# The last output group of a feed-forward stage moves into the hand-written order, outputs are issued in two parts, and vector work is asked for one turn sooner

## The chip, the cores and the metric

The kernel runs on one core of a Trainium2 chip. The engines named below are TensorE (PE, matrix products), VectorE (DVE), ScalarE (ACT), GpSimd (POOL) and SyncE (SP, which only issues the loads and stores here). The metric is the device time of one execution in microseconds (us). The kernel before takes 1966.19 us, the median of three runs that lie between 1964.42 and 1966.62.

## The reference

Two layers work on 512 latent tokens and 256 context tokens of 1024 channels. Each layer has an attention part (two kinds of attention, gated and projected) and then a feed-forward part. The change touches the feed-forward part alone, which in the reference is

```python
def swiglu(h, w_in, w_out):
    a, u = jnp.split(h @ w_in, 2, axis=-1)
    return (jax.nn.silu(a) * u) @ w_out
...
        h2 = modulate(rms_norm(x, norm2[l]), sh2, sc2)
        x = x + g2 * swiglu(h2, w_ffn_in[l], w_ffn_out[l])
        if not last:
            hc2 = modulate(rms_norm(ctx, norm2[l]), csh2, csc2)
            ctx = ctx + cg2 * swiglu(hc2, w_ffn_in[l], w_ffn_out[l])

    return rms_norm(x, final_norm)
```

`D_FF` is 2816. The first layer runs it over latent and context tokens together (768 columns in the kernel), the second over the 512 latent tokens alone. What follows is a norm: the next layer's first one, or the final one.

## The kernel before

**Numbers.** All data is 32-bit float. A product is made of three matmuls with halved operands: ACT copies a tile to the shorter matmul type (the *hi*), DVE subtracts the hi from the tile (the *lo*), and PE adds hi x hi, lo x hi and hi x lo in one PSUM bank. So every weight that is loaded costs an ACT copy and a DVE subtraction before PE can use it. In the trace the raw weight is `wr`, its halves are `wh` and `wl` (lines 366 and 368 for a weight split by the general helper, 1882 and 1886 for one split in the fixed order) or `w` (lines 1589 and 1593, for the quad's quarters).

**Layout.** Channels lie on the 128 partitions and tokens on the free axis. The 2816 hidden channels are 22 blocks `f` of 128, the 1024 output channels are 8 blocks `j`. The right-hand side, the normed tokens, is held in halves of `nh` columns: 384 in the first layer, 256 in the second.

**Hidden blocks.** `hidden(f)` makes gate and up projection of one block with `quad`, a scheme of Strassen's kind: seven turns of 12 matmuls in place of eight. The turns run in the order A11, A12, S1, S2, S4, S3, A22; their left operands are quarters of the weight or sums of quarters (S1, S2, S3, S4, made by DVE in `Quarters.sum`, lines 2124 to 2133). They use three PSUM banks, u, c, v, in the order u, c, v, u, v, u, u (`qu`, `qc`, `qv`). A bank goes on adding over its turns, and between two of them it must be read: ACT copies u after A11 (p1) and after S2 (u2), and v after S1 (v1), all at line 1732; DVE reads c after A12 (line 2152), v after S4 (again 2152) and u after S3 (line 2165, `tt<-qu,tt`) and after A22 (line 2169). Lines 1869 and 1870 then split the finished hidden block into `ph` and `pl`.

**Outputs.** After each chunk of four hidden blocks, `output` multiplies them with a 128x512 piece of the second weight (`wfo`) for each j, and DVE adds the gated result to the residual, `x<-po,G,x` (line 1581). Columns wider than one bank go in two spans. The last chunk has six blocks (`LAST`), so pieces of 128x768 and loads of 384 KB.

**Order.** In the middle of the feed-forward part, `paced` writes the order of PE, DVE and ACT by hand. It takes a list of steps (the turns and the outputs) and keeps four stages for them, load, sum, hi and lo, each some turns ahead of the step that PE is to run: lo three turns, hi four, sum five. Before it makes the sum of a step it makes sure that the lo of all steps up to two before it are written, because sums are made in place of quarters. The first step after a quad's S3 goes ahead of the quad's A22, so that there is other work between two turns on bank u. Loads go through SP's queue in the order in which they are issued, and hi and lo of an output live in three rotating buffers each.

**The last outputs.** Behind the part with the written order, the scheduler of the compiler's front end sets the order. The last chunk's outputs are made in two column groups (0 to 512 and 512 to 768 in the first layer, 0 to 256 and 256 to 512 in the second). The first group runs j = 0 to 7 and loads and splits one weight for each; the second runs j = 7 to 0, finds the last three weights still in their buffers, and loads and splits the other five again. With each residual a square is made and added up for the norm that follows (lines 484, 487 and 488); in the first layer the first group's x is also stored to `xd`.

## Time and profile before

One execution was profiled. It took 1967.19 us, 1.0 us more than the median; its span, from the first to the last instruction, is 1965.1 us, at a mean granted PE clock of 0.996.

| what | number |
| --- | --- |
| median of three runs | 1966.19 us |
| the profiled execution | 1967.19 us, span 1965.1 us |
| PE busy | 1920.8 us, 98% |
| DVE busy | 1479.8 us, 75% |
| ACT busy | 948.9 us, 48% |
| POOL busy | 220.1 us, 11% |
| loads of `wfo` for the last outputs | 26, 384 KB each, 3.3 us to landing |
| ACT's hi of such a weight, `wh` 128x768 | 26, 840 ns each |
| DVE's lo of such a weight, `wl` 128x768 | 26, 954 ns each |
| residual `x<-po,G,x` 128x512, 128x256 | 72 of 750 ns, 80 of 480 ns |

Times in rows of the trace are start and duration in microseconds, counted from the start of the span. `x12` groups twelve neighbours. What stands in square brackets is how long the engine stood idle ahead of the row, and which instruction ended that by the profile. Matmuls are pipelined: the next one starts before the row before it ends, so a pace is read from start to start. In the span's clock the hidden blocks of the first layer end near 1089, its last outputs run from there to 1138, and those of the second layer start near 1920.

### The profile page before, as it was taken

How to read it: one execution, taken by the hardware profiler on the slowest of the kernel's cores; microseconds unless marked ns; L12 is line 12 of the kernel's file. 1: busy time of each engine (PE TensorE's matmuls, PEld its weight loads, DVE VectorE, ACT ScalarE, POOL GpSimd, SP SyncE). 2: the span in 40 equal slices, each digit the busy share in tenths (PEclk: the TensorE clock that was granted, in tenths of full speed). 3: DMA queues.
4: the chain of work that ended last, by engine and by line, in shares of the span. 5: the costliest groups of instructions: out<-in, count | busy, mean ns of one | idle time of the engine just before them, and what ended most of it. 6: DMA issues, size and time to landing. Idle time of an engine off the chain costs nothing.

```text
span 1965.1 us, 31571 instructions
## 1 busy us (share of the span) xinstructions
PE 1920.8 (98%) x12298; PEld 1777.7 (90%) x12298; DVE 1479.8 (75%) x2813; ACT 948.9 (48%) x1832; POOL 220.1 (11%) x130
## 2 busy tenths in 40 slices
PE   8999999999999999999999999999999999999998
PEld 8989999888899999999999888889888999988997
DVE  7468887788768888786867587879566587876785
ACT  5456666642236534242524255667453364544454
POOL 0332212213200000000000013222300000000000
PEclk9999999999999999999999999999999999999999
DMA  8121112244452143434453422112235532233333
GB/s 324 44 71 41 52 57 63 76 148 166 144 207 86 65 132 127 124 107 138 137 161 116 129 86 60 52 49 78 67 93 196 176 112 77 95 112 96 94 109 108
DMA packets 73109, 214.78 MB, mean 109 GB/s; under 512 B 8704, under 2 KB 10880, under 8 KB 72960
## 3 DMA queue, kind: packets, MB, share of 16 engines
q1 hardware_dynamic: 72960, 212.78, 33.2%
q8 instruction: 96, 1.57, 0.3%
q14 instruction: 53, 0.43, 0.1%
HBM read 200.69 MB, written 6.82 MB: 106 GB/s over the span
## 4 chain that ended last, share of the span: by engine, by line
PE 66%; DVE 6%; issue 3%; ACT 2%; DMA 0%; POOL 0%; DVEq 0%; POOLq 0%; ACTq 0%
PE po L381 19%; PE qu L1726 13%; PE pj L381 10%; PE qv L1726 7%; PE pp L381 4%; PE qc L1726 3%; PE pf L381 3%; PE pv L954 1%; PE sc L1037 1%; PE y L1073 1%; PE tp L1063 1%; PE sc L1164 1%; PE y L1200 1%; DVE w L1593 1%; PE tp L1188 1%
## 5 line engine op out<-in xcount | busy, mean ns | idle before, releaser
L1726 PE MATMUL qu<-r,w 128*128 128x384 f32 (+1 forms) x1872 | 295.4, 310 | 1.9 <-ACT tt L1732 1.9
L1726 PEld LDWEIGHTS qu<-r,w 128*128 128x128 f32 x1872 | 281.1, 189 | 6.5 <-ACT tt L1732 2.7
L381 PE MATMUL pj<-h,wh 128*128 128x512 f32 (+1 forms) x704 | 257.5, 366 | 5.2 <-ACT kg L813 1.7
L366 ACT ACTIVATE wh<-wr 128x1024 fp32r<-128x1024 f32 (+2 forms) x157 | 146.1, 935 | 213.8 <-issue 67.2
L381 PE MATMUL pj<-h,wl 128*128 128x512 f32 (+1 forms) x704 | 247.6, 352 | 0.0
L381 PE MATMUL pj<-hl,wh 128*128 128x512 f32 (+1 forms) x704 | 247.0, 351 | 0.0
L381 PE MATMUL po<-ph,wh 128*128 128x512 f32 (+1 forms) x576 | 197.8, 344 | 2.6 <-ACT wh L366 1.6
L381 PE MATMUL po<-ph,wl 128*128 128x512 f32 (+1 forms) x576 | 196.4, 342 | 2.1 <-DVE wl L368 1.4
L381 PE MATMUL po<-pl,wh 128*128 128x512 f32 (+1 forms) x576 | 195.8, 340 | 0.0
L1589 ACT ACTIVATE w<-wr 128x512 fp32r<-128x512 f32 x234 | 145.4, 625 | 103.5 <-DVE wr L2129 39.3
L368 POOL TENSOR_TENSOR wl<-wr,wh 128x1024 fp32r<-128x1024 f32 (+1 forms) x66 | 144.6, 2194 | 392.8 <-ACT wh L366 392.7
L1581 DVE SCALAR_TENSOR_TENSOR x<-po,G,x 128x256 f32<-128x256 f32 (+3 forms) x168 | 99.1, 596 | 113.4 <-PE po L381 112.4
L1593 DVE TENSOR_TENSOR w<-wr,w 128x512 fp32r<-128x512 f32 x234 | 159.6, 685 | 14.9 <-ACT w L1589 13.6
L1726 PE MATMUL qv<-r,w 128*128 128x384 f32 (+1 forms) x936 | 151.1, 310 | 1.7 <-ACT tt L1732 1.7
L381 PEld LDWEIGHTS pj<-h,wh 128*128 128x128 f32 x704 | 134.0, 190 | 20.2 <-ACT kg L813 1.9
L381 PEld LDWEIGHTS pj<-h,wl 128*128 128x128 f32 x704 | 133.4, 189 | 18.2
L381 PEld LDWEIGHTS pj<-hl,wh 128*128 128x128 f32 x704 | 134.2, 191 | 13.8
L1726 PEld LDWEIGHTS qv<-r,w 128*128 128x128 f32 x936 | 141.1, 190 | 2.8 <-ACT tt L1732 2.7
L1013 ACT ACTIVATE pth<-tp 128x512 fp32r<-128x512 f32 x176 | 103.4, 595 | 65.3 <-PE tp L1063 37.7
L509 POOL TENSOR_TENSOR rs<-rs,expo 128x2 f32<-128x2 f32 (+2 forms) x8 | 6.2, 773 | 1116.7 <-DVE rs L508 1116.7
L1014 DVE TENSOR_TENSOR ptl<-tp,pth 128x512 fp32r<-128x512 f32 x176 | 119.5, 685 | 15.1 <-ACT pth L1013 13.4
L381 PEld LDWEIGHTS po<-ph,wh 128*128 128x128 f32 x576 | 108.4, 188 | 17.5 <-ACT wh L366 3.5
(249 smaller groups left out, 4321.2 us busy)
## 6 DMA issues: line engine op xcount, KB each, us to landing
wr<-wfi SPq DMA_DIRECT2D x88, 512.0 KB, 3.3
wr<-wmodT SPq DMA_DIRECT2D x84, 512.0 KB, 3.3
wr<-win SPq DMA_DIRECT2D x68, 512.0 KB, 3.3
wr<-wfo SPq DMA_DIRECT2D x64, 256.0 KB, 2.7
wr<-wo SPq DMA_DIRECT2D x26, 512.0 KB, 3.6
wr<-wfo SPq DMA_DIRECT2D x26, 384.0 KB, 3.3
wr<-wp SPq DMA_DIRECT2D x32, 256.0 KB, 2.9
x<-x SPq DMA_DIRECT2D x16, 384.0 KB, 6.4
```

The costliest lines, as they stand in the source:

```text
L366: nc.scalar.activation(hi, raw, AF.Copy)
L368: (eng or nc.gpsimd).tensor_tensor(lo, raw, hi[:].bitcast(F32), op=ALU.subtract)
L381: nc.tensor.matmul(ps[:, : b - a], u[:, c], v[k][:, a:b], start=(k == 0 and i == 0), stop=(k == nk - 1 and i == 2),)
L954: nc.tensor.matmul(ps[:, t * 256 : t * 256 + 256], a[k][:, tok], b[:, c], start=(k == 0 and i == 0), stop=(k == KB - 1 and i == 2))
L1013: nc.scalar.activation(hi, tp, AF.Copy)
L1014: nc.vector.tensor_tensor(lo, tp, hi[:].bitcast(F32), op=ALU.subtract)
L1037: nc.tensor.matmul(s[:, lo:up], qt[:, b * P : (b + 1) * P], kk[k][:, lo:up], start=(k == 0 and (b % 2 == 0 or lo > 0)), stop=(k == 1), ski ...
L1063: nc.tensor.transpose(tp[:, (2 * j + b) * P : (2 * j + b + 1) * P], ps_[b][:, (k + j) * P : (k + j + 1) * P], self.ident)
L1581: self.nc.vector.scalar_tensor_tensor(x[j][:, f:u], ps[:, f - a : u - a], self.G[l][i][:, s, j : j + 1], x[j][:, f:u], op0=ALU.mult, op1=A ...
L1589: self.nc.scalar.activation(t[:, :n], src, AF.Copy)
L1593: self.nc.vector.tensor_tensor(t[:, n : 2 * n], src, t[:, :n].bitcast(F32), op=ALU.subtract)
L1726: nc.tensor.matmul(banks[bank], u[:, c], v, start=(first and k == 0 and i == 0), stop=(k == kn - 1 and i == 2), skip_group_check=True)
```

## The change

There are three parts.

1. **When the stages of a step are due.** A table `goal` is made ahead of the loop. The lo is due as before. The hi of a step, and likewise its sum, is due when it was due before, or as soon as the stage after it is due one step later, whichever reaches further. And a stage `sum` of a step that makes no sum no longer forces the lo of the steps before it.

2. **Outputs in parts.** `outward` takes the place of `output`. A span of 512 columns becomes two steps, each with half of the matmuls over the hidden blocks in the same bank; the residual follows the second. The step that goes between S3 and A22 is thus half an output. For the last chunk the first two outputs are cut after 3, 5 and 6 of the six hidden blocks, and the third parts, which need the last hidden block, are put behind.

3. **The last outputs.** The first column group is now part of the steps that `paced` orders. Its weights j = 0 to 4 (`KEPT`) get slots of their own in a larger pool, so all eight are still there for the second group, which loads and splits nothing. The squares are made through `summed`. The second group is written as before, without the loads.

Per layer this takes out five loads of 384 KB, five ACT copies and five DVE subtractions. The matmuls are the same ones.

```diff
--- before.py
+++ after.py
@@ -32,6 +32,8 @@
 FB = FF // P
 
 CHUNK, LAST = 4, 6
+KEPT = 5
 EPS = 1e-6
 QSCALE = -(HD ** -0.5)
 BIG = 3.0e38
@@ -1758,6 +1760,12 @@
         for s in steps:
             at.append(at[-1] + s.cost)
         order = "load", "sum", "hi", "lo"
+        last = len(steps)
+        upto = lambda n, t: max(n + 1, next((i for i in range(n, last) if at[i] >= at[n] + t), last))
+        goal = dict(lo=[upto(n, 3 * near + 0.1) for n in range(last)])
+        for stage, after, t in (("hi", "lo", 4), ("sum", "hi", 5)):
+            goal[stage] = [max(upto(n, t * near + 0.1), goal[after][min(n + 1, last - 1)]) for n in range(last)]
         done = dict.fromkeys(order, 0)
         share = min(1.0, 1.2 * sum(c for c, *_ in beside) / sum(s.cost - s.busy for s in steps))
         free, wait, since = 0.0, [], 0.0
@@ -1767,7 +1775,7 @@
         def go(stage, up):
             while done[stage] < up:
                 n = done[stage]
-                if stage == "sum":
+                if stage == "sum" and steps[n].sum:
                     go("lo", n - 2)
                 if stage != "load":
                     go(order[order.index(stage) - 1], n + 1)
@@ -1793,14 +1801,13 @@
             self.live += 1
 
         for n, s in enumerate(steps):
-            ahead = lambda t: max(n + 1, next((i for i in range(n, len(steps)) if at[i] >= at[n] + t), len(steps)))
             first, late, later = late, later, []
-            go("lo", ahead(3 * near + 0.1))
+            go("lo", goal["lo"][n])
             for run in first:
                 run()
-            go("hi", ahead(4 * near + 0.1))
-            go("sum", ahead(5 * near + 0.1))
-            far = ahead(5 * near + LEAD)
+            go("hi", goal["hi"][n])
+            go("sum", goal["sum"][n])
+            far = upto(n, 5 * near + LEAD)
             while done["load"] < far and (not steps[done["load"]].load or self.live <= 2):
                 go("load", done["load"] + 1)
             free = min(free + (s.cost - s.busy) * (share if ready() else 1.0), BEHIND)
@@ -1869,32 +1876,52 @@
                 lambda: nc.scalar.activation(hi[:, : 2 * nh], src, AF.Copy),
                 lambda: nc.vector.tensor_tensor(lo[:, : 2 * nh], src, hi[:, : 2 * nh].bitcast(F32), op=ALU.subtract)]
 
-        def output(chunk, j):
-            n = CHUNK * P
+        def outward(chunk, j, spans, own=False, then=None, cuts=None):
+            kn = CHUNK if chunk < last_chunk else LAST
+            n = kn * P
             w, banks = {}, {}
 
             def load():
-                w["raw"] = self.raw(d["wfo"][l, j, :, chunk * n : (chunk + 1) * n], n)
+                w["raw"] = self.raw(d["wfo"][l, j, :, chunk * CHUNK * P : chunk * CHUNK * P + n], n)
                 self.live += 1
 
+            def half(tag):
+                return self.slot(tag, F32R) if own else self.wpool.tile([P, n], F32R, tag=tag, name=self.name(tag))
             def upper():
-                w["hi"] = self.wpool.tile([P, n], F32R, tag="wh", name=self.name("wh"))
+                w["hi"] = half("wh")
                 nc.scalar.activation(w["hi"], w["raw"], AF.Copy)
 
             def lower():
-                w["lo"] = self.wpool.tile([P, n], F32R, tag="wl", name=self.name("wl"))
+                w["lo"] = half("wl")
                 nc.vector.tensor_tensor(w["lo"], w["raw"], w["hi"][:].bitcast(F32), op=ALU.subtract)
                 self.live -= 1
 
-            def mul(a, b):
-                banks[a] = self.ps("a", "po")[:, : b - a]
-                drain(self.steps(banks[a], (w["hi"], w["lo"]), second[chunk], a, b, CHUNK))
-            return [
-                Step(3 * CHUNK * ((b - a) * COL + FIX), (0.0 if a else busy(n)) + busy(b - a) + 0.06,
-                     lambda a=a, b=b: mul(a, b), lambda a=a, b=b: self.residual(l, 1, banks[a], x, j, a, b),
-                     gated=True, **({} if a else dict(load=load, hi=upper, lo=lower)))
-                for a, b in spans]
+            def mul(a, b, up):
+                if a not in banks:
+                    ps = self.ps("a", "po")[:, : b - a]
+                    banks[a] = ps, self.steps(ps, (w["hi"], w["lo"]), second[chunk], a, b, kn)
+                for _ in range(up):
+                    next(banks[a][1], None)
+            def take(a, b):
+                self.residual(l, 1, banks[a][0], x, j, a, b)
+                return then(j, a, b) if then else None
+            steps = []
+            for a, b in spans:
+                at = 0
+                for up in cuts or ((kn // 2, kn) if b - a == S else (kn,)):
+                    first, end = not steps, up == kn
+                    cost = busy(n) * first + (busy(b - a) + 0.06 + (busy(b - a) if then else 0.0)) * end
+                    steps.append(Step(
+                        3 * (up - at) * ((b - a) * COL + FIX), cost, lambda a=a, b=b, n=up - at: mul(a, b, n),
+                        (lambda a=a, b=b: take(a, b)) if end else lambda: None, gated=True,
+                        **(dict(load=load, hi=upper, lo=lower) if first else {})))
+                    at = up
+            return steps, w
 
         def rest():
 
@@ -1903,13 +1930,35 @@
             for f in range(len(early) // 2, FB):
                 parts = [hidden(f)]
                 if f % CHUNK == 1 and CHUNK < f < FB - CHUNK // 2:
-                    parts.append([s for j in range(KB) for s in output(f // CHUNK - 1, j)])
+                    parts.append([s for j in range(KB) for s in outward(f // CHUNK - 1, j, spans)[0]])
                 for some in parts:
                     end = some[-1:] if some is parts[0] else []
                     some = some[: len(some) - len(end)]
                     steps += some[:1] + tail + some[1:]
                     tail = end
-            return steps + tail
+            for j in range(KB):
+                some, ws[j] = outward(last_chunk, j, groups[:1], j < KEPT, summed, (3, LAST - 1, LAST) if j < 2 else None)
+                steps += some[:1] + tail + some[1:-1] if j == 0 else some[:-1] if j == 1 else some
+                tail = some[-1:] if j == 0 else []
+                if j == 1:
+                    steps += last + some[-1:]
+                last = some[-1:]
+            return steps
+        def summed(j, a, b):
+            if l < DEPTH - 1:
+                nc.sync.dma_start(self.xd[j][:, a:b], x[j][:, a:b])
+            t = pool.tile([P, S], F32, tag="sq" if acc else "acc", name=self.name("sq"))[:, : b - a]
+            acc.append(t)
+            todo = [(1, lambda: nc.scalar.activation(t, x[j][:, a:b], AF.Square))]
+            if j:
+                todo.append((2, lambda: nc.vector.tensor_tensor(acc[0], acc[0], t, op=ALU.add)))
+            return todo
+        last_chunk = (FB - LAST) // CHUNK
+        ws, acc = {}, []
 
         early, cover = EARLY[l], COVER[l]
         order = [(*part, half) for half in range(2) for part in early[:cover]]
@@ -1930,29 +1979,22 @@
         order = {getattr(mybir.EngineType, e) for e in ("PE", "DVE", "Activation")}
         with self.tc.manual_schedule(engines=order):
             self.paced(rest(), 3 * KB // 2 * (nh * COL + FIX), beside, lambda: self.gated)
-        chunk = (FB - LAST) // CHUNK
-        ws = {}
-        for i, (a, b) in enumerate(groups):
-            acc = None
-            for at, j in enumerate(list(range(KB))[:: 1 - 2 * i]):
-                if i == 0 or at >= 3:
-                    ws[j] = self.weight(d["wfo"][l, j, :, chunk * CHUNK * P :], LAST * P, nc.vector)
-                w = ws[j]
-                ps = self.ps("a", "po")[:, : b - a]
-                drain(self.steps(ps, w, second[chunk], a, b, LAST))
-                self.residual(l, 1, ps, x, j, a, b)
-                if l < DEPTH - 1 and i == 0:
-                    nc.sync.dma_start(self.xd[j][:, a:b], x[j][:, a:b])
-                if l == DEPTH - 1 and i == 1 and at >= KB - 2:
-                    acc = [acc] if at == KB - 2 else acc
-                    acc.append(pool.tile([P, S], F32, tag="sq", name=self.name("sq")))
-                    nc.scalar.activation(acc[-1][:, : b - a], x[j][:, a:b], AF.Square)
-                else:
-                    acc = self.square(x[j], a, b, pool, acc)
-            done(acc, a, b)
+        done(acc[0], *groups[0])
+        a, b = groups[1]
+        acc = None
+        for j in reversed(range(KB)):
+            ps = self.ps("a", "po")[:, : b - a]
+            drain(self.steps(ps, (ws[j]["hi"], ws[j]["lo"]), second[last_chunk], a, b, LAST))
+            self.residual(l, 1, ps, x, j, a, b)
+            if l == DEPTH - 1 and j < 2:
+                acc = [acc] if j else acc
+                acc.append(pool.tile([P, S], F32, tag="sq", name=self.name("sq")))
+                nc.scalar.activation(acc[-1][:, : b - a], x[j][:, a:b], AF.Square)
+            else:
+                acc = self.square(x[j], a, b, pool, acc)
+        done(acc, a, b)
 
     def run(self):
         nc, tc, d = self.nc, self.tc, self.d
```

Where the written order differs is seen best on DVE and ACT. First DVE at the hand-over from the outputs to the next quad in the second layer. `x<-po` is a residual, `ws<-wr` and `wr<-ws,wr` are the sums, `wr<-wr` (lines 2133 and 2175) is the sum S4, and `w` are lo. Before:

```order
L2129 TENSOR_TENSOR wr_17618<-ws_17676,wr_17618 128x512
L1581 SCALAR_TENSOR_TENSOR x_16044<-po_17686,G_1_114,x_16044 128x512
L1593 TENSOR_TENSOR w_17678<-ws_17676,w_17678 128x512
L1593 TENSOR_TENSOR w_17701<-wr_17618,w_17701 128x512
L2133 TENSOR_TENSOR wr_17618<-wr_17618 128x512
L1593 TENSOR_TENSOR w_17705<-wr_17618,w_17705 128x512
L2152 TENSOR_TENSOR tt_17720<-qc_17725,tt_17720 128x256
```

The same place with the change:

```order
L2171 TENSOR_TENSOR wr_17588<-ws_17638,wr_17588 128x512
L1595 TENSOR_TENSOR w_17648<-ws_17638,w_17648 128x512
L2175 TENSOR_TENSOR wr_17588<-wr_17588 128x512
L1583 SCALAR_TENSOR_TENSOR x_16014<-po_17656,G_1_114,x_16014 128x512
L1595 TENSOR_TENSOR w_17664<-wr_17588,w_17664 128x512
L1595 TENSOR_TENSOR w_17675<-wr_17588,w_17675 128x512
L2194 TENSOR_TENSOR tt_17690<-qc_17695,tt_17690 128x256
```

The sum S4 has moved ahead of the last output's residual and of the lo of S2.

Next ACT in the last quad of the first layer, where the last outputs begin. `tt<-qv` and `tt<-qu` are the copies of the banks v (v1) and u (u2), `wh` are the hi of the last outputs' weights. Before:

```order
L1589 ACTIVATE w_11103<-wr_10964 128x512
L2153 ACTIVATE ph_11118<-tt_11081 128x384
L1589 ACTIVATE w_11123<-wr_10964 128x512
L1732 ACTIVATE tt_11138<-qv_11125 128x384
L366 ACTIVATE wh_11203<-wr_11201 128x768
L1732 ACTIVATE tt_11153<-qu_11068 128x384
L366 ACTIVATE wh_11232<-wr_11230 128x768
```

The same place with the change:

```order
L1591 ACTIVATE w_11095<-wr_10958 128x512
L2195 ACTIVATE ph_11112<-tt_11070 128x384
L1895 ACTIVATE wh_11117<-wr_11097 128x768
L1734 ACTIVATE tt_11132<-qv_11119 128x384
L1591 ACTIVATE w_11136<-wr_10958 128x512
L1734 ACTIVATE tt_11160<-qu_11057 128x384
L2195 ACTIVATE ph_11112<-tt_11160 128x384
L1895 ACTIVATE wh_11179<-wr_11138 128x768
```

The first `wh` has moved ahead of the copy of v, and the second behind the work on the copy of u.

Last, DVE at the start of the second column group in the first layer. Before:

```order
L1581 SCALAR_TENSOR_TENSOR x_6218<-po_11493,G_1_112,x_6218 128x256
L368 TENSOR_TENSOR wl_11565<-wr_11561,wh_11563 128x768
L1581 SCALAR_TENSOR_TENSOR x_6216<-po_11515,G_1_112,x_6216 128x256
L368 TENSOR_TENSOR wl_11594<-wr_11590,wh_11592 128x768
L508 TENSOR_SCALAR rs_11445<-st_11440 128x4
```

The same place with the change:

```order
L1583 SCALAR_TENSOR_TENSOR x_6218<-po_11493,G_1_112,x_6218 128x256
L370 TENSOR_TENSOR wl_11700<-wr_11696,wh_11698 128x1024
L1583 SCALAR_TENSOR_TENSOR x_6216<-po_11515,G_1_112,x_6216 128x256
L370 TENSOR_TENSOR wl_11706<-wr_11702,wh_11704 128x1024
L510 TENSOR_SCALAR rs_11445<-st_11440 128x4
```

The second splits of `wfo` (128x768) are gone, and the first weights of the next layer (128x1024) stand in their place.

## The prediction

> **What bounds the kernel now.** I read the page's busy shares first, then the places where TensorE (PE) waits, and there the timelines of PE, VectorE (DVE) and ScalarE (ACT) side by side.
>
> ```profile
> PE 1920.8 (98%) x12298; PEld 1777.7 (90%) x12298; DVE 1479.8 (75%) x2813; ACT 948.9 (48%) x1832; POOL 220.1 (11%) x130
> ```
>
> PE is busy for 98% of the span, and the change leaves every matmul as it is. All that it can win or lose is time in which PE stands still. Of that only the places count whose neighbours on PE, DVE or ACT the change moves: the hand-over from outputs to quad in layer 1, and the last outputs of both layers.
>
> The hand-over comes four times in layer 1. Here is the first, PE, then DVE, then ACT, and then the PE groups that hold the waits of all four (window 1683 to 1882):
>
> ```profile
> 1680.43 1.60 PE L1726 MATMUL qu<-r,w 128*128 128x256 f32 x12
> 1681.87 1.60 PE L1726 MATMUL qc<-r,w 128*128 128x256 f32 x12
> 1683.31 1.60 PE L1726 MATMUL qv<-r,w 128*128 128x256 f32 x12
> 1685.38 1.70 PE L1726 MATMUL qu<-r,w 128*128 128x256 f32 x12 [0.48 <-ACT tt L1732]
> 1687.41 1.69 PE L1726 MATMUL qv<-r,w 128*128 128x256 f32 x12 [0.34 <-ACT tt L1732]
> 1688.94 0.28 PE L1726 MATMUL qu<-r,w 128*128 128x256 f32 x1
> ...
> 1681.76 0.74 DVE L1581 SCALAR_TENSOR_TENSOR x<-po,G,x 128x512 f32<-128x512 f32 x1
> 1682.42 0.68 DVE L1593 TENSOR_TENSOR w<-ws,w 128x512 fp32r<-128x512 f32 x1
> 1683.02 0.69 DVE L1593 TENSOR_TENSOR w<-wr,w 128x512 fp32r<-128x512 f32 x1
> 1683.62 0.69 DVE L2133 TENSOR_TENSOR wr<-wr 128x512 f32<-128x512 f32 x1
> 1685.09 0.69 DVE L1593 TENSOR_TENSOR w<-wr,w 128x512 fp32r<-128x512 f32 x1 [0.78 <-ACT w L1589]
> ...
> 1684.43 0.63 ACT L1589 ACTIVATE w<-wr 128x512 fp32r<-128x512 f32 x1 [1.86 <-DVE wr L2133]
> 1684.96 0.37 ACT L1732 ACTIVATE tt<-qu 128x256 f32<-128x256 f32 x1
> 1687.00 0.36 ACT L1732 ACTIVATE tt<-qv 128x256 f32<-128x256 f32 x1
> ...
> L1726 PE MATMUL qu<-r,w 128*128 128x256 f32 x588 | 78.0, 285 | 1.9 <-ACT tt L1732 1.9
> L1726 PE MATMUL qv<-r,w 128*128 128x256 f32 x305 | 41.2, 284 | 1.3 <-ACT tt L1732 1.3
> ```
>
> The first two PE rows give the pace: 12 matmuls of 256 columns in 1.44 us, 0.12 each. The turn at 1683.31 should be followed at 1684.75; it is followed at 1685.38. PE waits for ACT's copy of bank u at 1684.96, but that copy is itself behind an ACT row (hi of S4, 1684.43) which had waited 1.86 us for DVE's sum S4 (1683.62). So DVE's order is the cause. The sum stands behind the residual of the last output (1681.76) and the lo of S1 and S2 (1682.42, 1683.02). What is needed soonest comes last. The copy of bank v (1687.00) is late for the same reason one turn on.
>
> **The change part by part.** I price a wait by starts, not by the idle column: the time from one start to the next, less the matmuls in between at their pace. That also takes in the slower first turn after a wait (1687.41 to 1688.94 is 1.53, 0.09 over the pace).
>
> *A, the sums a turn earlier.* From 1683.31 to 1688.94 are 5.63 us for three turns of 1.44, so 1.31 are lost. The group rows show 1.9 and 1.3 us idle in the window of four hand-overs, which is 4 times 0.48 and 0.34, so the four are alike: 4 x 1.31 = **5.2 us**. In the new order the residual and the lo of S2 stand behind the sum of S4. Start to start these took 0.66 (1681.76 to 1682.42) and 0.60 (1683.02 to 1683.62), so the sum, hi of S4 and the copy of u come 1.26 earlier; 0.63 is needed. The copy of v, moved by the same 1.26, starts at 1685.74 and ends at 1686.10; the turn after next writes v again at 1683.31 + 2 x 1.44 = 1686.19, so that one fits with only 0.09 to spare. The bounds: 0 (the lateness only moves) and 5.2. I take 5.2, since the first shift is twice what is needed and 1.26 counts only two of the rows that go from ahead of the sum. What is late next is the lo of S2 and the residual: the residual frees a bank of the outputs that are over by then. DVE's work is only reordered here.
>
> *B, last outputs in the fixed order, five weights kept.* Per layer five loads of 384 KB on SP's queue, five hi on ACT and five lo on DVE go; PE's matmuls stay. None of that saved work is on the path by itself, so it is worth only the waits that it ends. These are the last outputs of layer 0, start and second column group, and the first matmuls of layer 1:
>
> ```profile
> 1086.74 2.27 PE L1726 MATMUL qu<-r,w 128*128 128x384 f32 x12
> 1089.99 0.50 PE L381 MATMUL po<-ph,wh 128*128 128x512 f32 x1 [0.98 <-ACT wh L366]
> 1097.74 0.39 PE L381 MATMUL po<-pl,wh 128*128 128x512 f32 x1
> 1089.10 0.84 ACT L366 ACTIVATE wh<-wr 128x768 fp32r<-128x768 f32 x1 [9.90 <-issue]
> ...
> 1134.38 0.28 PE L381 MATMUL po<-pl,wh 128*128 128x256 f32 x1
> 1136.08 0.39 PE L381 MATMUL po<-ph,wl 128*128 128x256 f32 x1 [1.42 <-DVE wl L368]
> 1136.31 0.28 PE L381 MATMUL po<-ph,wh 128*128 128x256 f32 x1
> 1137.96 0.28 PE L381 MATMUL po<-ph,wl 128*128 128x256 f32 x1
> 1139.42 0.47 PE L381 MATMUL pj<-h,wh 128*128 128x512 f32 x1 [1.18 <-ACT sq L487]
> ...
> 1135.08 0.95 DVE L368 TENSOR_TENSOR wl<-wr,wh 128x768 fp32r<-128x768 f32 x1
> 1138.80 0.48 DVE L1581 SCALAR_TENSOR_TENSOR x<-po,G,x 128x256 f32<-128x256 f32 x1
> ```
>
> Start of the group: the turn at 1086.74 has 12 matmuls of 384 columns, 2.08 us (709.03 to 711.11, below), yet the next matmul starts at 1089.99: 3.25 - 2.08 = 1.17. From there to 1097.74 are 29 matmuls of 512 columns at 0.233 (711.11 to 711.34), 6.76 of 7.75 us: 0.99 more. ACT stood idle for 9.90 us before the hi (1089.10) with no data missing: it waited for one of three hi buffers, which PE frees only when an output ends. With five slots of their own the hi wait for nothing but their load. **2.2 us**, bounds 0 and 2.2; I take it whole, because 9.9 us of idle ACT stand before it.
>
> Second group: 1134.38 to 1136.08 is 1.70, less 0.12, and 0.11 in the next one: **1.7 us**. It waits for a lo (1135.08) that no longer exists. Bounds 0 and 1.7; I take all.
>
> Layer 1's first matmul: 1.46 - 0.12 = **1.3 us**. The row names an ACT square, but this matmul reuses a PSUM bank, and the residual at 1138.80 that empties such a bank ends at 1139.28, 0.14 before the start; ACT is said to release, but it is DVE, queued behind splits, that ends last. Without five lo of 0.95 DVE comes there earlier. Bounds 0 and 1.3; I take 0.8, as the hl that these matmuls need stand in the same queue.
>
> The last outputs of layer 1 (the last row is the waits view's: what PE waited for there, us in total, times, longest):
>
> ```profile
> 1920.37 0.28 PE L381 MATMUL po<-pl,wh 128*128 128x256 f32 x1
> 1921.59 0.50 PE L381 MATMUL po<-ph,wh 128*128 128x256 f32 x2 [0.94 <-ACT ph L1869]
> 1924.20 0.28 PE L381 MATMUL po<-ph,wl 128*128 128x256 f32 x1
> 1926.46 0.28 PE L381 MATMUL po<-ph,wh 128*128 128x256 f32 x1
> 1923.98 2.31 ACT L366 ACTIVATE wh<-wr 128x768 fp32r<-128x768 f32 x3 [2.44 <-PE po L381]
> PE po L381 <- ACT wh L366: 0.6, 2, 0.4
> ```
>
> 1920.37 to 1921.59 is 1.22, less 0.12: 1.10, for the hi of the last hidden block. 1924.20 to 1926.46 is 2.26 for six matmuls (0.72): 1.54, while three hi that had waited 2.44 for a buffer run one behind the other (1923.98). Together **2.6 us**. The second part goes with the slots. The first depends on cover: now the last block's matmuls stand behind 9 + 6 + 15 others of 256 columns, 30 x 0.12 = 3.6 us, of which 21 x 0.12 = 2.5 us follow A22. In these rows the chain behind A22 takes 1.34 us to the end of the hi (A22's turn ends one matmul, 0.12, before 1920.37, and PE goes on at 1921.59), and a lo of 0.69 as in A's rows follows: 2.0, and 0.5 is left of the cover, less than one split of a weight (0.95) that may stand between. I take half of the 1.10, 0.55, with bounds 0 and 1.1.
>
> *C, outputs in two parts.* After S3 only half an output now covers the read of bank u, which A22 writes again. At a chunk's first output in layer 0:
>
> ```profile
> 709.03 2.24 PE L1726 MATMUL qu<-r,w 128*128 128x384 f32 x12
> 711.11 0.39 PE L381 MATMUL po<-ph,wh 128*128 128x512 f32 x1
> 711.34 0.40 PE L381 MATMUL po<-pl,wh 128*128 128x512 f32 x1
> 711.52 0.55 DVE L2165 TENSOR_TENSOR tt<-qu,tt 128x384 f32<-128x384 f32 x1
> ```
>
> Half an output is 6 x 0.233 = 1.40 us, so A22 may start at 711.11 + 1.40 = 712.51; DVE's read ends at 712.07. The margin is 0.44, where a whole output left 1.84. There are ten such places (four chunks and the last group, in each layer). Bounds: nothing, or a wait of 1.8 each (the third rival). I put 0.10 on each, the size of one restart: **-1.0**.
>
> *D, a wait added.* The hi of the first last output now stands ahead of ACT's copy of v in the last quad, and ACT's queue behind it (that copy, hi of A22, the copies of u) would wait for the load.
>
> ```profile
> 1073.72 0.49 ACT L1732 ACTIVATE tt<-qv 128x384 f32<-128x384 f32 x1 [0.44 <-PE qv L1726]
> 1074.11 0.84 ACT L366 ACTIVATE wh<-wr 128x768 fp32r<-128x768 f32 x1
> ```
>
> Before, the copy started at 1073.72 and the hi right after it. Swapped, the copy comes at most 0.84 later if the load has landed, ending near 1075.0; v is written again one turn of 2.08 after its end at about 1073.6, near 1075.7. So 0, with bounds 0 and 1 us. SP has fewer loads, so nothing queues longer there.
>
> *Sum.* 5.2 + 2.2 + 1.7 + 0.8 + (1.54 + 0.55) - 1.0 = **11.0 us**. The profiled execution took 1967.19 for its span of 1965.1, 1.0 above the median of 1966.19. Against the median: 1966.2 - 11.0 = **1955.2 us**.
>
> The Trainium skill, Perfetto Trace Analysis, section Identifying the Most-Contended Engine, says that matmul busy time is no good measure of headroom, since pipelined PE instructions look different in a trace. The rows bear it out: 0.98 idle at 1089.99 was 1.17 by starts. By the idle column alone the waits would be 3.2 + 1.0 + 1.4 + 1.2 + 0.9 and 0.6 us, 8.3 in all; less the same allowances of 2.1 the forecast would be 1960.0.
>
> **The rivals.** *R1: the hand-over stays late (the change doesn't do what it says there).* The sum of S4 now has to wait for something else, its own inputs or the hi of A12. For it: DVE is 75% busy, and 0.78 idle at 1685.09 shows a ping-pong of ACT and DVE that a new order need not end. Against it: a shift of 1.26 where 0.63 is enough. Price 5.2: 1955.2 + 5.2 = **1960.4**.
>
> *R2: the last groups win nothing.* PE runs through the first wait and stands at the next: the loads or the residuals end last in place of the buffers. For it: the last outputs' lo stay on DVE (0.95 against 18 x 0.12 = 2.2 us of matmuls per output in layer 1, and 0.48 for x). Against it: ACT's 9.90 and 2.44 idle for buffers alone. Then only A and C remain, 5.2 - 1.0: **1962.0**.
>
> *R3, slower: half an output is no cover.* If in the new order the read of bank u stands behind three more vector rows of 0.60 to 0.66 start to start, it ends some 1.9 later, and A22 waits 1.9 - 0.44 plus 0.09 restart, about 1.6 at each of ten places: 16 us against the 12.0 that the rest brings, 1966.2 - 12.0 + 16 = **1970**. It decides from 1.2 us per place. For it: the margin of 0.44. Against it: in the new order the read follows that of bank v with no split between, and the row at 711.52 was behind a long reduction already.
>
> **How the numbers follow.** Forecast 0.62, R1 0.15, R2 0.15, R3 0.05, and 0.03 for a gain above all of my bounds. Within the forecast the allowances alone make 1952.9 (all 13.1 us by starts, no new wait) to about 1958. The range that leaves out 2 in 10 reaches over R1 to R2: **1952.0 to 1962.5**. A measurement of this kernel can tell some 0.2%, 3.9 us, from no change: faster is below 1962.3. The forecast, R1 and nearly half of R2 lie there: 0.83. The rest of R2 and mild forms of R3: same 0.12. Slower 0.05.
>
> **What would show it.** *A:* the turn after qv starts 1.44 after it at all four hand-overs, and the PE groups of that window have no idle behind ACT's tt. *B:* no PE row of the last groups names a wh or wl of 128x768; the waits of 1.4 and 1.2 at the layer's end are gone or under half. *C:* A22's first matmul after half an output has no idle named by DVE's tt. The prediction is wrong if PE's waits at A22 sum to over 3 us, if the hi of the last hidden block still holds PE for 1 us, or if waits appear in layer 1's attention, which I take as untouched.

## The result and the profile after

The changed kernel takes 1952.68 us, the median of four runs (1951.61 to 1953.08), against 1965.31 us for the kernel before. The ratio is 0.9935, with a 95% interval of 0.9923 to 0.9946: 12.6 us less, where 11.0 were predicted. (The kernel before itself came out 0.9 us below the 1966.19 from which the prediction counted.) The profiled execution took 1951.61 us for a span of 1949.8. In the page's first part PE's share is the same 98%, of a shorter span:

```profile
PE 1913.9 (98%) x12298; PEld 1776.4 (91%) x12298; DVE 1472.4 (76%) x2803; ACT 943.3 (48%) x1822; POOL 220.2 (11%) x130
```

**The hand-over in layer 1.** The same place as in the prediction, timeline of PE and then DVE, and the groups of PE in the window of all four hand-overs (1674 to 1873):

```profile
1674.02 1.60 PE L1728 MATMUL qc<-r,w 128*128 128x256 f32 x12
1675.46 1.60 PE L1728 MATMUL qv<-r,w 128*128 128x256 f32 x12
1676.90 1.60 PE L1728 MATMUL qu<-r,w 128*128 128x256 f32 x12
1678.34 1.60 PE L1728 MATMUL qv<-r,w 128*128 128x256 f32 x12
1679.78 0.40 PE L1728 MATMUL qu<-r,w 128*128 128x256 f32 x2
...
1673.19 0.69 DVE L2175 TENSOR_TENSOR wr<-wr 128x512 f32<-128x512 f32 x1
1673.79 0.74 DVE L1583 SCALAR_TENSOR_TENSOR x<-po,G,x 128x512 f32<-128x512 f32 x1
...
L1728 PE MATMUL qu<-r,w 128*128 128x256 f32 x614 | 81.1, 285 | 0.3 <-DVE tt L2207 0.3
L1728 PE MATMUL qv<-r,w 128*128 128x256 f32 x312 | 41.7, 283 | 0.0
```

In this place turn follows turn after 1.44 us. The sum S4 (line 2175 now) starts at 1673.19, 2.27 us ahead of the start of qv's turn at 1675.46; before, it started at 1683.62, 0.31 behind that of qv's turn. No wait behind ACT's copies is left in the window. The 0.3 that stands there is a new wait of another kind, below.

**The last outputs of layer 0 and the start of layer 1.** PE at the start of the last outputs and at the layer's end, and ACT in the last quad:

```profile
1083.81 0.51 PE L1728 MATMUL qu<-r,w 128*128 128x384 f32 x2
1084.15 0.39 PE L383 MATMUL po<-ph,wh 128*128 128x512 f32 x1
1134.33 0.28 PE L383 MATMUL po<-ph,wl 128*128 128x256 f32 x1
1134.45 0.40 PE L383 MATMUL pj<-h,wh 128*128 128x512 f32 x1
...
1073.12 0.85 ACT L1895 ACTIVATE wh<-wr 128x768 fp32r<-128x768 f32 x1 [0.15 <-DMA wr<-wfo]
1073.93 0.49 ACT L1734 ACTIVATE tt<-qv 128x384 f32<-128x384 f32 x1
```

The first matmul behind A22 and layer 1's first one follow at PE's pace (0.34 for two matmuls of 384 columns, 0.12). The waits view of PE is empty for the last outputs of both layers (1075 to 1140 and 1898 to 1930). The added wait of the hi for its load was 0.15 us long, and the copy of v behind it was done at 1074.42, more than 1 us ahead of its turn. So the term D of the prediction is nothing, as taken.

**Half an output as cover.** PE and DVE at the first chunk's outputs in layer 0:

```profile
711.03 0.39 PE L383 MATMUL po<-ph,wh 128*128 128x512 f32 x1
712.42 2.25 PE L1728 MATMUL qu<-r,w 128*128 128x384 f32 x12
711.23 0.56 DVE L2207 TENSOR_TENSOR tt<-qu,tt 128x384 f32<-128x384 f32 x1 [0.31 <-PE qu L1728]
```

The read of bank u starts 0.20 after the turn of S3 and is done at 711.79; A22 starts at 712.42 without a wait, 0.63 later. None of the ten half-output places shows one.

**New waits, elsewhere.** They stand at quads with no outputs next to them: three in layer 0 (761, 776, 791) and one in layer 1 (1820). PE and DVE at the first, and PE at the last:

```profile
761.82 2.35 PE L1728 MATMUL qu<-r,w 128*128 128x384 f32 x12 [0.34 <-DVE tt L2207]
760.07 1.22 DVE L451 CUSTOM_DVE_ANT_0 wr<-wr,crow 128x1024 f32<-128x1024 f32 x1
761.21 0.55 DVE L2207 TENSOR_TENSOR tt<-qu,tt 128x384 f32<-128x384 f32 x1
1820.12 1.70 PE L1728 MATMUL qu<-r,w 128*128 128x256 f32 x12 [0.32 <-DVE tt L2207]
```

In layer 0 a reduction for the modulation (line 451, 1.22 us) now stands right ahead of the read of bank u at all three, and A22 waits for the read behind it. The waits are not all new: by starts fourteen plain quads of layer 1 lose 0.23 each at the same read in the kernel before, 3.3 in all, too little per place for the idle column to show. With the change thirteen still do, and the one at 1820 loses 0.58.

**By starts, place by place.** In us, each wait with its restart, from the starts of PE's rows as in the prediction:

| place | lost before | prediction's gain | lost after |
| --- | --- | --- | --- |
| four hand-overs, layer 1 | 5.3 | 5.2 | 0 |
| last outputs of layer 0, start | 2.2 | 2.2 | 0 |
| second group, layer 0 | 1.7 | 1.7 | 0 |
| first matmuls of layer 1 | 1.4 | 0.8 | 0 |
| last outputs of layer 1 | 2.7 | 2.1 | 0 |
| first chunk's outputs, layer 0 (722) | 0.8 | none | 0 |
| A22 after half an output | 0 | -1.0 | 0 |
| A22 at plain quads, added | 0 | none | 1.7 |

The gains are 14.1, less 1.7: 12.4 us, against 12.6 between the medians. The two profiled executions lie further apart, 15.6 us; most of the rest goes with PE's clock after waits that the change does not touch (last section).

### The profile page after: what moved, and what is told of

It reads as the page before. It is cut to its first block, busy times and chain, and to the rows that moved or that the text cites. A ratio compares the mean times of both kernels' runs of the same rounds, so it can differ in the third digit from the quotient of the medians.

```text
span 1949.8 us, 31497 instructions
## 1 busy us (share of the span) xinstructions
PE 1913.9 (98%) x12298; PEld 1776.4 (91%) x12298; DVE 1472.4 (76%) x2803; ACT 943.3 (48%) x1822; POOL 220.2 (11%) x130
## 4 chain that ended last, share of the span: by engine, by line
PE 68%; DVE 5%; issue 2%; ACT 1%; DMA 0%; POOL 0%; DVEq 0%; POOLq 0%; ACTq 0%
PE po L383 21%; PE qu L1728 13%; PE pj L383 11%; PE qv L1728 7%; PE pp L383 4%; PE qc L1728 3%; PE pf L383 3%; PE pv L956 1%; PE y L1075 1%; PE sc L1039 1%; PE tp L1065 1%; PE sc L1166 1%; PE y L1202 1%; PE tp L1190 1%; DVE m L1047 0%
## 5 line engine op out<-in xcount | busy, mean ns | idle before, releaser
L368 ACT ACTIVATE wh<-wr 128x1024 fp32r<-128x1024 f32 (+1 forms) x131 | 124.6, 954 | 178.2 <-issue 41.3
L1595 DVE TENSOR_TENSOR w<-wr,w 128x512 fp32r<-128x512 f32 x234 | 159.3, 685 | 11.5 <-ACT w L1591 10.5
L383 PEld LDWEIGHTS po<-ph,wl 128*128 128x128 f32 x576 | 108.3, 188 | 14.1 <-DVE wl L1899 0.2
```

Source lines behind the costliest of these rows:

```text
L368: nc.scalar.activation(hi, raw, AF.Copy)
L383: nc.tensor.matmul(ps[:, : b - a], u[:, c], v[k][:, a:b], start=(k == 0 and i == 0), stop=(k == nk - 1 and i == 2),)
L1595: self.nc.vector.tensor_tensor(t[:, n : 2 * n], src, t[:, :n].bitcast(F32), op=ALU.subtract)
```

## The experiments

Ratios are to the kernel before on the same chip, with their 95% intervals. The changed kernel was timed a second time beside three of the experiments. Three chips were used. The kernel before took 1965.7 us on the one of e1 to e4, 1965.6 on that of c_change, e5, e8 and e9, and 1964.1 on that of e6, e7, e10 and e11. So where one of the last four is set against the change, two chips are compared, and on the change's the kernel before took 1.2 us longer.

> The changed kernel once more, for comparison on the chip of the next three. 12.6 us below before, ratio 0.9936.

Measured: 1952.67 us, 0.9935 (0.9922 to 0.9947), the same as the first time.

**What cures the hand-over?** First each of the two parts alone, put on the kernel before.

> The kernel before with the first part of the change alone (the table that asks for hi and sum sooner); outputs whole, last outputs as before. In its order the sum S4 stands ahead of the last residual, as in the change. Theory: DVE's order is the cause of the late hand-overs in layer 1, and any order with S4 ahead of the residual cures them. Then the four hand-overs lose nothing, 5.2 us less than before, about 1960.2 against 1965.3, and the last groups' waits stay. Rival: the sum stays late for its own inputs and the lateness moves; then within 1 us of before.

```diff
+        goal = dict(lo=[upto(n, 3 * near + 0.1) for n in range(last)])
+        for stage, after, t in (("hi", "lo", 4), ("sum", "hi", 5)):
+            goal[stage] = [max(upto(n, t * near + 0.1), goal[after][min(n + 1, last - 1)]) for n in range(last)]
...
-                if stage == "sum":
+                if stage == "sum" and steps[n].sum:
```

Measured: 1961.19 us, 0.9975 (0.9966 to 0.9983), 4.5 us less.

> The kernel before with the second part alone: outputs of 512 columns in two steps, no new table, last outputs as before. Here too S4 stands ahead of the last residual, since the ends of the outputs come one step later. Theory (order of DVE is all that counts, so this part cures the hand-over as well as the first): 5.2 us less, 1960.1, and new waits of A22 after half an output of at most 0.1 each. Rival one: only the table cures it, no change. Rival two: half an output is no cover, eight waits of 0.5 or more, 1964 or slower.

```diff
+                for up in (CHUNK // 2, CHUNK) if b - a == S else (CHUNK,):
+                    first, end = not steps, up == CHUNK
+                    steps.append(Step(
+                        3 * (up - at) * ((b - a) * COL + FIX), busy(n) * first + (busy(b - a) + 0.06) * end,
...
```

Measured: 1960.49 us, 0.9973 (0.9962 to 0.9984), 5.2 us less. PE's first group in the window of the hand-overs, in the first kernel and then in the second:

```profile
L1726 PE MATMUL qu<-r,w 128*128 128x256 f32 x636 | 83.9, 284 | 0.0
```

```profile
L1726 PE MATMUL qu<-r,w 128*128 128x256 f32 x648 | 85.5, 284 | 0.0
```

Either part alone ends the hand-over's waits. What the two kernels share is DVE's order, with S4 ahead of the last residual (1680.67 and 1681.28 in the first, 1678.98 and 1679.58 in the second). Of the 0.8 lost at 722 the first kernel still loses 0.25, the second nothing. Then the table was taken out of the change.

> The changed kernel without its first part, the table of due stages. The orders of PE and ACT are then the very same and DVE's differs in one pair of rows: in the last quad of layer 1 the read of bank u (tt<-qu) stands behind the lo of the second last output in place of ahead of it. Theory (the parts alone cure the hand-over, the table only moves this read): the four hand-overs still lose nothing; the read starts one lo later (0.95) where the cover is 9 x 0.12 = 1.08 us, so A22 waits once for 0.5 to 0.9: at most 1 us above the change. Rival, as in the prediction (the table is what moves the sum): the hand-over's 5.2 us come back.

```diff
-            go("hi", goal["hi"][n])
-            go("sum", goal["sum"][n])
+            go("hi", ahead(4 * near + 0.1))
+            go("sum", ahead(5 * near + 0.1))
```

Measured: 1953.72 us, 0.9937 (0.9924 to 0.9951), not to be told from the change by its time. Its trace shows the one wait that was expected, PE and DVE in the last quad of layer 1:

```profile
1904.97 1.21 PE L1728 MATMUL qu<-r,w 128*128 128x256 f32 x8 [0.57 <-DVE tt L2202]
1904.50 0.42 DVE L2202 TENSOR_TENSOR tt<-qu,tt 128x256 f32<-128x256 f32 x1
```

By starts it is 0.74 us, 0.85 with the restart. So beside the other two parts the table is worth that and no more; the outputs in parts move the sum. The rival, that the sum is late without the table, falls. The other way round:

> The changed kernel with the outputs of the four-block chunks whole again; the table and the fixed order of the last outputs stay. Theory: the table alone puts S4 ahead of the last residual, so the four hand-overs lose nothing, and the cover of A22 is longer: within 1 us of the change. Rival: the parts are what cures the hand-over beside the last outputs in the fixed order: 5 us above the change.

```diff
-                for up in cuts or ((kn // 2, kn) if b - a == S else (kn,)):
+                for up in cuts or (kn,):
```

Measured: 1956.62 us, 0.9967 (0.9954 to 0.9979), some 4 us above the change's median, and 5 when each is set against the kernel before on its own chip (7.5 below it, where the change is 12.6 below), where within 1 was expected. The hand-overs are clean here as well, so this is not the rival. The loss stands in one place in the main, layer 1's first matmul:

```profile
1136.20 0.77 PE L383 MATMUL pj<-h,wh 128*128 128x512 f32 x1 [2.39 <-DVE x L1583]
```

It waits for a residual that the front end's scheduler put behind three rows of DVE that make `hl` (a half of the next layer's input) in place of two. By starts the wait is 2.55, and the matmuls behind it run at half pace, which costs 1.5 us more. Another 0.25 is lost at 722, while the three waits of layer 0's plain quads (1.4) are gone, so that by starts the kernel loses about 3 more than the change; the rest of the 5 stays open. So the whole outputs are not at fault themselves: the part behind the written one is the same code here, and the scheduler ordered it in another way.

**What cures the last groups, the slots or the order?**

> The changed kernel without the slots: the first group stays in the fixed order, but its weights rotate through the three buffers and the second group loads and splits five of them again. Theory: the waits for buffers come back, 3.0 at layer 0's end and 2 to 3.7 at the first groups: 5 to 6.7 us above the change, 1957.7 to 1959.4. Rival: the fixed order alone cures the first groups and only the second group's 3.0 come back: 1955.7.

```diff
-                some, ws[j] = outward(last_chunk, j, groups[:1], j < KEPT, summed, ...)
+                some, ws[j] = outward(last_chunk, j, groups[:1], False, summed, ...)
...
         for j in reversed(range(KB)):
+            if j < KEPT:
+                hi, lo = self.weight(d["wfo"][l, j, :, last_chunk * CHUNK * P :], LAST * P, nc.vector)
```

Measured: 1955.76 us, 0.9951 (0.9939 to 0.9963), 3 us above the change. That is the rival. All that PE waits for in the last outputs of layer 0 and the start of layer 1, by the waits view (us in total, times, longest):

```profile
PE po L383 <- DVE wl L370: 1.4, 1, 1.4
PE pj L383 <- DVE wl L370: 0.2, 1, 0.2
```

With three rotating buffers the first groups have no wait at all, in either layer. What is back is the wait for a split in layer 0's second group, and a short one at layer 1's first matmuls. My theory that the number of buffers held the first groups falls. The hi for which PE had waited shows what the order did. Here are PE's A22 and that hi in this kernel, and then the last hi of the group in e11_squares_last (below), which also waits for one of the three buffers and where the profile names the releaser:

```profile
1083.05 2.26 PE L1728 MATMUL qu<-r,w 128*128 128x384 f32 x12
1085.39 0.85 ACT L1895 ACTIVATE wh<-wr 128x768 fp32r<-128x768 f32 x1 [4.39 <-issue]
```

```profile
1090.10 0.85 ACT L368 ACTIVATE wh<-wr 128x768 fp32r<-128x768 f32 x1 [8.29 <-PE qu L1728]
```

The hi starts 0.08 after the end of A22 (1085.31); in the kernel before it was 0.09 (1089.10 after 1089.01). The halves of a quad rotate through the same three buffers as those of the outputs (line 1588), so it is A22 that frees this one. In the old order all 30 matmuls of two outputs that can run without the last hidden block stood ahead of A22. In the written order 9 of them stand ahead of it and 21 behind, and PE has these 21 to run while the split is made. Whether A22's place alone is the cure was not tried by itself.

The slots alone were the counterpart:

> The kernel before with the weights j = 0 to 4 of the last outputs in slots of their own and no second load of them; the front end's scheduler still sets the order of the first group. Theory: what holds PE in the last groups is buffers and the second split, so the waits of 1.4 and 1.2 at the end of layer 0, the 2.2 at its last outputs and the 1.5 of layer 1's go, only the 1.1 for the last hidden block's hi stays: 6.7 us less, 1958.6. Rival: the fixed order is what cures the first groups, the slots only the second: 3.0 us less, 1962.3.

```diff
-                if i == 0 or at >= 3:
-                    ws[j] = self.weight(d["wfo"][l, j, :, chunk * CHUNK * P :], LAST * P, nc.vector)
+                if i == 0:
+                    ws[j] = self.weight(d["wfo"][l, j, :, chunk * CHUNK * P :], LAST * P, nc.vector, own=j < 5)
```

Measured: 2001.78 us, 1.0184 (1.0171 to 1.0197): 36 us slower, far outside of what either theory gave. The waits of PE and of SP's queue in layer 0's last outputs, and two neighbours on ACT there:

```profile
PE po L383 <- ACT wh L368: 11.8, 4, 5.1
SPq L1949 <- DVE x L1583: 23.6, 4, 14.4
1110.53 0.63 ACT L489 ACTIVATE sq<-x 128x512 f32<-128x512 f32 x1 [4.47 <-DVE x L1583]
1111.07 0.83 ACT L368 ACTIVATE wh<-wr 128x768 fp32r<-128x768 f32 x1
```

The two views are of the stretches 1080 to 1125 and 1070 to 1122. The scheduler wrote ACT's order so that a square, which waits for the residual of one output, stands ahead of the hi of a later one, and SP's so that stores of x stand ahead of loads. So an output's weight is not split before the output ahead of it is done. The waits are not the whole loss: the granted clock is 0.83 from 1085 to 1135 and 0.77 from 1935 to 1965, where the kernel before has 1.00 in the same stages, so PE also runs at half pace behind some of them. To see whether it is the squares:

> The kernel e3_slots_only, which lost 36 us, with the squares of the first column group written behind its eight outputs in place of one behind each. Theory of e3's loss: on ACT's queue each square, which waits for a residual, stood ahead of the hi that a later output needed, so loading, splitting and multiplying went one output at a time. Then it is gone here, and slots alone bring what was expected of them: the waits of 1.4 to 2.2 at layer 0's end and 1.5 in layer 1 go, about 1959. Rival: the loads came late because raw buffers or slots came free late: then most of the 36 us stay, 1985 or more.

```diff
-                else:
+                elif i:
                     acc = self.square(x[j], a, b, pool, acc)
+            if i == 0:
+                for j in range(KB):
+                    acc = self.square(x[j], a, b, pool, acc)
```

Measured: 1961.69 us, 0.9988 (0.9979 to 0.9996). Of the 36 us none is left, and the first groups of both layers are free of waits, without the written order. On SP the stores now stand behind all loads as well, so for layer 0 squares and stores are not told apart; layer 1's first group has no stores, waited for its hi in e3_slots_only too (8.0 us) and is free here, so there it is the squares. It is 2.4 us below the kernel before on its chip, where 6.3 were expected, for the reason met above: its one wait in this stage is that of layer 1's first matmul for a residual. By starts it is 2.4, with 1.6 for the half pace behind it, where the kernel before lost 1.4 at that place.

```profile
PE pj L383 <- DVE x L1583: 2.3, 1, 2.3
```

So the first groups can be cured in two ways: the written order with three buffers, or slots with the squares behind the outputs. Slots with the squares in between are worse than nothing.

**What does the half output cost?**

> The changed kernel without any output between S3 and A22 at the eight places where a chunk's outputs begin (the last groups keep theirs). Theory: in the change's trace the read of bank u there starts 0.20 after S3's end and takes 0.56 (0.42 in layer 1), so without cover A22 waits 0.76 and 0.10 more for the restart in layer 0, 0.62 and 0.10 in layer 1: 4 x 0.86 + 4 x 0.72 = 6.3 us above the change, 1959.0. That is the price of the prediction's third rival at its worst, without rows queued ahead. Rival: the bank needs longer, or rows queue ahead of the read, over 10 us.

```diff
-                    steps += some[:1] + tail + some[1:]
+                    steps += some[:1] + tail + some[1:] if some is parts[0] or end else tail + some
```

Measured: 1959.48 us, 0.9977 (0.9968 to 0.9986), 6.8 us above the change's median where 6.3 were expected, and 8.0 when each is set against the kernel before on its own chip. By starts the eight places lose 6.8. One of them, PE and DVE:

```profile
712.64 1.68 PE L1728 MATMUL qu<-r,w 128*128 128x384 f32 x8 [0.65 <-DVE tt L2207]
712.02 0.56 DVE L2207 TENSOR_TENSOR tt<-qu,tt 128x384 f32<-128x384 f32 x1 [0.32 <-PE qu L1728]
```

Without cover A22 waits 0.8 in layer 0 and 0.7 in layer 1, and 0.1 for the restart. Half an output (1.40) is more than is needed.

**The new waits.** Two ways to get the reductions out of the read's way, and a third with what they taught.

> The changed kernel with one more rule: in the step of S3 no reduction for the modulation is put in, so the read of bank u after S3 no longer stands behind one (1.22 us). Theory: the three new waits of A22 in layer 0 (0.62, 0.37 and 0.37 by starts) came from that and go, 1.3 us below the change; the waits of layer 1 stay. Rival: the reductions held back land ahead of another read and cost as much: no difference.

```diff
-            if wait and at[n] - since >= LEAD and free >= 0.5 * wait[0][0]:
+            if wait and not s.hold and at[n] - since >= LEAD and free >= 0.5 * wait[0][0]:
```

Measured: 1953.87 us, 0.9937 (0.9925 to 0.9950): no gain. The three waits are gone, and one of 1.9 by starts (2.2 with the slower starts behind it) is new, at the first outputs of layer 0:

```profile
721.82 0.50 PE L383 MATMUL po<-ph,wh 128*128 128x512 f32 x1 [1.70 <-ACT wh L1895]
```

The reductions that were held back must be done before the first residual, so they run there one behind the other, and the weights' split waits behind them. This was the rival.

> The kernel e8_hold with the read of bank u moved ahead of the sums S3 and S2 of the next quad as well. Theory: in layer 1 the read ends 0.1 to 0.3 late in 14 plain quads (0.13 wait and 0.10 restart each) because it stands behind two sums (0.72 and 0.61 start to start); with it first these waits go too: 3.2 us and the 1.3 of e8_hold, 4.5 below the change, about 1948. Rival: the sums, now 0.4 later, make the copies or S4 late, and the gain is lost or turns to a loss of up to 14 x 0.5 us.

```diff
-            go("sum", goal["sum"][n])
+            if not s.hold:
+                go("sum", goal["sum"][n])
...
             for delay, run in s.take() or ():
                 (late if delay == 1 else later).append(run)
+            if s.hold:
+                go("sum", goal["sum"][n])
```

Measured: 1953.18 us, 0.9933 (0.9920 to 0.9945), again no gain that can be told. In its trace layer 1's waits of A22 are all gone, the small ones at the fourteen plain quads too; the first outputs of layer 0 cost 3.7 by starts, of which 1.7 are a slow clock (below).

> The changed kernel with the sums S3 and S2 put behind the read of bank u after S3, and the reductions left where the change has them (not held back as in e8_hold and e9_read_first). Theory: the reductions held back piled up ahead of the first outputs of layer 0 and cost there 2 to 3 us what they had saved; left in place, with 1.3 us of sums out of the read's way, the waits of A22 go in both layers and nothing piles up: 1.1 in layer 0 and 14 x 0.23 + 0.35 = 3.6 in layer 1, 4.7 below the change, 1948.0. Rival: the read behind a reduction alone is still late in layer 0, and only layer 1's 3.6 go: 1949.1. Second rival: the waits of e9_read_first at the first outputs come from the sums and not from the reductions: 1950 or more.

Its edit is that of e9_read_first without the one of e8_hold. Measured: 1948.46 us (1946.92 to 1951.13), 0.9927 (0.9913 to 0.9940): 15.7 us below the median of before on its chip, where the change is 12.6 to 12.9 below on its two; by the ratio it is 14 us. The intervals of the two ratios overlap, so the times alone do not settle that it beats the change; the trace does for its part. PE and DVE at a plain quad of layer 1, and PE's one wait at a quad of layer 0:

```profile
1814.74 4.48 PE L1728 MATMUL qu<-r,w 128*128 128x256 f32 x36
1816.38 0.42 DVE L2210 TENSOR_TENSOR tt<-qu,tt 128x256 f32<-128x256 f32 x1
1046.95 0.44 PE L1728 MATMUL qv<-r,w 128*128 128x384 f32 x1 [1.10 <-ACT tt L1734]
```

Three turns of u run through without a wait: 36 matmuls of 0.12 are 4.32, and the last one's row is 0.16 longer than its pace. By starts it loses as much as the change in layer 0 and 3.5 less from the first quads of layer 1 to the end (7.0 against 10.5); 4.7 were expected. What is missing is the wait at 1046.95 (1.4 with its restart), which no other kernel shows and which takes back layer 0's gain; what makes it was not tried.

## Why the prediction was right, and where not

*The total.* 1955.2 was forecast, 1952.7 measured, inside the range of 1952.0 to 1962.5. The working by starts held: place by place the sum came out at 12.4, and by the idle column alone the forecast would have been 1960.0. That 12.4 lies so near to 11.0 is in part luck. An allowance of 1.0 was not needed, two of 0.5 were not either, and a gain of 0.8 was not foreseen; new waits of 1.7 at places where none was looked for stand against these. Two slips in the prediction's numbers change nothing: all 13.1 us off 1966.2 make 1953.1 and not 1952.9, and the 0.03 for a gain above all bounds belongs to the chance for faster. The sentence of the Trainium skill on matmul busy time (Perfetto Trace Analysis, Identifying the Most-Contended Engine) is borne out by PE's share, which is 98% before and after, though 12.6 us went.

*A, the hand-over.* The cause (DVE's order, S4 behind the residual) and the size (5.2 against 5.3) were right. The credit was half wrong: the step was put down to the sums being asked for a turn earlier, which is the table's work. The table alone does cure the hand-over (e1_sums_only), but so do the outputs in parts alone (e2_parts_only, e5_no_sums), and beside them the table is worth 0.85. R1 is out.

*B, the last outputs.* The places and sizes were right, the two allowances of 0.5 not needed: the boundary gave its whole 1.4, and the wait for the last hidden block went whole, as the cover of 2.5 was enough. The mechanism was half wrong. "With five slots of their own the hi wait for nothing but their load" was offered as the cure of the first groups, on ACT's 9.90 us of idle. That idle was for a buffer, but the reading that "PE frees only when an output ends" was wrong: the hi starts as A22 ends, and no output of the group had ended by then. With the same three buffers and the written order, which brings A22 forward, there is no wait (e4_no_slots). The slots are worth the second group and the boundary, 3 us. The reading of layer 1's first matmul holds: where the wait of 1.18 stands in e1_sums_only, the profile names the residual (DVE x) and no longer the square. R2 is out, but e3_slots_only shows the thing that it named, the next wait taking over, in a kernel that has the slots and not the order.

*C, half an output.* The sign was right by accident. The allowance of 1.0 stood at ten places that lose nothing; the margin was put at 0.44 and is 0.63, since the read there waits for PE alone now. R3 is out, since no read at these ten places stands behind more rows; with no cover at all eight of them cost 6.8 us by starts (e7_no_cover), and it decides from 12. The 1.7 that was lost came at four plain quads, in three of them because a reduction now stands ahead of the read: with these held back the three waits are gone (e8_hold). One sign of being wrong that the prediction named did come, if it is counted by starts: A22's waits sum to 5.0, over 3. But 3.3 of them stood at layer 1's plain quads before as well, which the prediction had not seen. The step that failed is the one which looked for R3's mechanism (the read of bank u queued on DVE) only where the cover was cut, and not at the plain quads, where rows were moved in front of the read.

*The first outputs of layer 0.* A gain of 0.8 at 722 was not in the prediction at all. It is partly a matter of the execution: e3_slots_only and e11_squares_last leave the code of this stage as it was before, and lose 0.44 and 0.34 there. PE waited for a lo that DVE had behind the last reductions, and these waited for a load. The reduction in question, before and then with the change:

```profile
717.91 1.23 DVE L449 CUSTOM_DVE_ANT_0 junk<-wr,crow 128x1024 f32<-128x1024 f32 x1 [1.67 <-DMA wr<-wmodT]
```

```profile
716.25 1.23 DVE L451 CUSTOM_DVE_ANT_0 junk<-wr,crow 128x1024 f32<-128x1024 f32 x1 [0.98 <-DMA wr<-wmodT]
```

The reduction starts 1.7 us sooner, and all that is behind it on DVE moves up. The prediction took the reductions and their loads as fixed, the same omission as under C. Which of the moved rows made the load start sooner was not tried.

## What to carry to other kernels

When one engine is the bound, price each wait from start to start and find which row of the feeding engine's queue stands ahead of the one that is needed; moving that row may be done by several edits, and only undoing each one alone tells which did it. An engine that idles for a buffer is no proof that more buffers help: here the order alone ended the wait, and more buffers under an order that a scheduler made afresh cost 36 us. And a row that is moved away from one critical read lands ahead of another, so look for the same dependence at all places that the rows move to.

## What the hardware showed unasked

PE ran at half pace for some 3.5 us after some waits of 1.7 to 2.4 us. Here is e9_read_first at the first outputs of layer 0, PE and then the windows view (PE busy and its count, the other engines, the granted clock as the third number from the end):

```profile
724.08 0.59 PE L383 MATMUL po<-ph,wh 128*128 128x512 f32 x1 [1.84 <-ACT wh L1898]
725.83 0.63 PE L383 MATMUL po<-pl,wh 128*128 128x512 f32 x1
726.25 0.63 PE L383 MATMUL po<-ph,wl 128*128 128x512 f32 x1
727.53 0.50 PE L383 MATMUL po<-ph,wl 128*128 128x512 f32 x1
727.87 0.39 PE L383 MATMUL po<-ph,wh 128*128 128x512 f32 x1
728.11 0.40 PE L383 MATMUL po<-pl,wh 128*128 128x512 f32 x1
715.00:720.00 5.00, 5.00 (x30) 4.33 (x29) 3.19 (x5) 0.00 (x0) 0.00 (x0) 1.00 0.46 144
724.00:727.00 3.00, 2.92 (x7) 2.10 (x8) 2.94 (x5) 1.07 (x3) 0.00 (x0) 0.56 0.34 87
```

After 1.84 us of idle the matmuls of 512 columns follow each other after 0.42 (725.83 to 726.25) in place of 0.24 (727.87 to 728.11), and the granted clock from 724 to 727 is 0.56, where it was 1.00 from 715 to 720. It lasts until about 727.53, 3.5 us after the wait. The Trainium skill (TensorE: Matmul & The Clock Gate, Part 1: The HAM clock gate) tells of a gate that closes to half after an idle window of about 3.4 us and opens after a busy one. The half pace and its length agree; the wait that closed it is only half as long as that window, so by the measurement a shorter one can be enough.

It is not so each time. One wait in layer 1's attention, the same in all kernels, in the kernel before and then in the changed one:

```profile
1204.38 2.68 PE L1037 MATMUL sc<-kk,q 128*128 128x512 f32 x8 [1.66 <-ACT p L1053]
```

```profile
1199.35 1.68 PE L1039 MATMUL sc<-kk,q 128*128 128x512 f32 x8 [1.66 <-ACT p L1055]
```

Equal idle, equal matmuls, and 1.0 us between them. Around it the granted clock by windows is 0.97 before and 1.00 after, and likewise at 400 to 450 and (not shown) at 1250 to 1300:

```profile
400.00:450.00 50.00, 48.31 (x290) 42.79 (x289) 43.94 (x72) 18.23 (x36) 12.04 (x8) 0.97 0.48 165
1200.00:1250.00 50.00, 47.99 (x330) 43.88 (x329) 37.69 (x88) 32.01 (x65) 8.77 (x4) 0.97 0.13 38
```

```profile
400.00:450.00 50.00, 48.31 (x300) 43.05 (x299) 43.91 (x74) 19.23 (x39) 12.93 (x8) 1.00 0.46 160
1200.00:1250.00 50.00, 49.65 (x344) 45.16 (x343) 39.51 (x89) 33.78 (x67) 9.84 (x5) 1.00 0.11 38
```

In 50 us 0.03 of the clock is 1.5 us. The first 50 us are the other way round, 1.00 before and 0.97 after. Three places for and one against make 3 us, which is what the profiled executions lie further apart than the medians. The change leaves the code at these places as it is. What decides whether a wait closes the gate was not settled; two single executions of one kernel can differ by as much as a small change brings.
